# Loading the first k-tile in four transfers and holding back the fourth k-tile's load, in a two-layer decoder trunk

## The chip, the cores and the metric

The kernel runs on one core of a Trainium2 chip. The metric is the device time of one execution in microseconds (us), the median of several runs. The engines' names in the profile are PE (TensorE, the matmuls; PEld is its loading of weights), DVE (VectorE), ACT (ScalarE), POOL (GpSimd) and SP (SyncE, which here only issues transfers). A name with a q behind it (SPq, ACTq) is the engine's sequencer, which issues transfers and waits.

## What is computed

The reference is a decoder trunk of two layers on 256 tokens of 1024 features, in float32. In each layer a token mixer is followed by a dense MLP, and each of the two is added to its scaled input and normalised:

```
for i in range(DEPTH):                      # DEPTH = 2
    mix = moba_attention(h, ...) if i == 0 else dilated_attention(h, ...)
    h = layer_norm(ALPHA * h + mix, ...)
    h = layer_norm(ALPHA * h + square(relu(h @ w_in)) @ w_out, ...)
```

Layer 0 has 16 heads of causal attention (with 256 tokens there is one block of keys, so each query sees its own block alone); layer 1 has 12 heads in three groups of dilated windows. The MLP is 4096 wide. What matters here is the very first piece of work: `x @ w_qkv`, of which the first six blocks of 128 output columns, rotated later into queries and keys, are computed from a combined table `xw0` that holds, for each of the eight k-tiles of 128 features, the 256 columns of the transposed activations and then 768 columns of weights, 1024 columns in all (512 KB).

## The kernel before, in words

All matmuls keep nearly the precision of float32 with three products: each operand is split into a rounded part hi and the rest lo, and hi by hi, hi by lo and lo by hi are summed in PSUM. So each tile of weights that is loaded (`raw`) is first converted to hi (a copy that rounds, mostly on ACT, L355, or on DVE, L357) and then to lo (a subtraction on DVE, L360). The activations of a k-tile are converted in the same way into `xs`.

The start of the program is in the class `Stage` (L383), one object for each of the eight k-tiles of `xw0`. `STAGE_PARTS` (L54) says, for the first, second, third and all later k-tiles: into which parts the 1024 columns are cut (part 0 is the 256 columns of activations, the others are blocks of weights, given by the block at which each ends), which engine rounds each part of weights, and which parts are loaded by one transfer on which queue (SP's or ACT's). Before, the first k-tile is cut after weight blocks 1, 3 and 6; parts 0 and 1 (384 columns, 192 KB) come by one transfer on SP's queue, parts 2 and 3 (640 columns, 320 KB) by one on ACT's. The second k-tile comes half by SP and half by ACT, the third in two halves by SP, all later ones in a single transfer of 512 KB by SP. K-tiles 0 to 3 land in buffers of the tag `raw`; later ones borrow the buffers of `g`, `b` and `tok`.

The loop at L606 then makes 18 matmuls for each k-tile: three terms for each of six blocks of weights, into three PSUM banks (`acc`). Ahead of them stand dummy matmuls of 512 columns on constants (`WARM`, L60, eight of them, and `idle`, L455), which keep TensorE busy until data come; one more of 256 columns stands behind the first real matmul.

All operations are recorded with what they read and write, and then set into an order by a planner (`Plan.order`, L163) that simulates the engines with costs and due times. Each engine works off its own list in that order, and semaphores hold an instruction back until what it reads has been written. Transfers on one queue go out in the order in which they are issued; a transfer whose completion semaphore is still in use by an earlier one waits for that one to land (eight such semaphores take turns). SP's list at the start is: the first k-tile's part, the second's, two of the third, then the k-tiles four to eight, the rope table, two tiles of `wqk0`, and then all later weights.

Of the kernel before, what the change touches and what calls it, by code (L numbers as in the profile page):

```python
# [47 lines left out]
NFIRST = 6  # L48
PER = 1024 // (NFIRST * P)

STAGE_HOME = (("raw", NRAW),) * 4 + (("g", 1), ("b", 1)) + (("tok", 2),) * 2


STAGE_PARTS = (  # L54
    ((1, 3, NFIRST), ("DVE", "ACT", "ACT"), ((0, 1, "SP"), (2, 3, "ACT"))),
    ((2, NFIRST), ("DVE", "ACT"), ((0, 1, "SP"), (2, 2, "ACT"))),
    ((2, NFIRST), ("ACT", "ACT"), ((0, 1, "SP"), (2, 2, "SP"))),
    ((NFIRST,), ("ACT",), ((0, 1, "SP"),)),
)
WARM = (512,) * 8  # L60

# [51 lines left out]
class Plan:  # L115
# [16 lines left out]
    def op(self, eng, cost, fn, reads=(), writes=(), xfer=0.0, early=0.0, ahead=0.0):  # L132
        o = Op()
        o.n, o.eng, o.cost, o.fn, o.xfer = len(self.ops), eng, cost, fn, xfer
        o.early, o.ahead = early, ahead
        o.preds, o.succs, o.bufs = set(), [], set()
        for group, is_write in ((reads, False), (writes, True)):
            for item in group:
                b, key = item if isinstance(item, tuple) else (item, None)
                o.bufs.add(b)  # L140
                for k, st in b.state.items():
                    if key is None or k is None or k == key:
                        if st[0] is not None:
                            o.preds.add(st[0])
                        if is_write:
                            o.preds.update(st[1])
                st = b.state.setdefault(key, [None, []])
                if is_write:
                    if key is None:
                        b.state = {None: [o, []]}  # L150
                    else:
                        st[0], st[1] = o, []
                else:
                    st[1].append(o)
        o.preds.discard(o)
        for p in o.preds:
            p.succs.append(o)
        for b in o.bufs:
            b.left += 1
        self.ops.append(o)  # L160
        return o
# [133 lines left out]
def tile_trunk(  # L295
# [22 lines left out]
    nc = tc.nc  # L318
    plan = Plan()
    op = plan.op  # L320
# [5 lines left out]
    class Bufs:  # L326
        def __init__(self, pl, bufs):
            self.pl, self.bufs = pl, bufs
# [4 lines left out]
    def mk(shape, dt, tag, bufs, space=None):  # L333
        uid[0] += 1
        return plan.buf(Bufs(space or sb, bufs), shape, dt, tag, bufs, f"{tag}_{uid[0]}")

    def psum(tag):
        return mk([P, 512], F32, tag, 4, ps_pool)
# [14 lines left out]
    def split(n, src, hi, lo, r, whi, wlo, sbuf=False, hi_eng="ACT"):  # L353
        if hi_eng == "ACT":
            op("ACT", act(n, sbuf=sbuf), lambda: nc.scalar.activation(hi(), src(), AF.Copy), r, whi)  # L355
        else:
            op("DVE", dve(n), lambda: nc.vector.tensor_copy(hi(), src()), r, whi)  # L357
        op(
            "DVE", dve(n),
            lambda: nc.vector.tensor_tensor(lo(), src(), f32(hi()), op=ALU.subtract), list(r) + list(whi), wlo,  # L360
        )

    def mm(out_ap, lhsT, rhs, start, stop):
        nc.tensor.matmul(out_ap, lhsT, rhs, start=start, stop=stop)  # L364
# [16 lines left out]
    xs = [mk([P, 4, 2, S], F32R, f"xs{i}", 1) for i in range(2)]  # L381

    class Stage:  # L383


        def __init__(self, kt, hi, lo):
            self.kt, self.hi, self.lo = kt, hi, lo
            self.raw = mk([P, D], F32, *STAGE_HOME[kt])
            ends, self.engines, loads = STAGE_PARTS[min(kt, len(STAGE_PARTS) - 1)]
            cuts = [S] + [S + n * P for n in ends]  # L390
            self.parts = list(zip([0] + cuts[:-1], cuts))
            for first, last, eng in loads:
                self.load(self.parts[first][0], self.parts[last][1], tuple(range(first, last + 1)), eng)
            a, k = kt // 4, kt % 4
            keys = [(kt, m) for m in range(2)]
            split(
                S, lambda: self.raw.t[:, :S], lambda: xs[a].t[:, k, 0, :], lambda: xs[a].t[:, k, 1, :],
                [(self.raw, 0)], [(xs[a], (0, *m)) for m in keys], [(xs[a], (1, *m)) for m in keys], sbuf=True,
            )
            for i, (c0, c1) in list(enumerate(self.parts))[1:]:  # L400
                src = slice(c0, c1)
                dst = slice(self.col(0) + c0 - S, self.col(0) + c1 - S)
                split(
                    c1 - c0, lambda src=src: self.raw.t[:, src], lambda dst=dst: hi.t[:, dst],
                    lambda dst=dst: lo.t[:, dst], [(self.raw, i)], [(hi, (kt, i))], [(lo, (kt, i))], sbuf=True,
                    hi_eng=self.engines[i - 1],
                )
# [47 lines left out]
    def idle(n, reads=()):  # L455
        ones = nc.const_aps.tensor
        op(
            "PE", n / 2400, lambda: mm(idle_ps.t[:, :n], ones(1.0, [P, P], BF16), ones(1.0, [P, n], BF16), True, True),
            list(reads), [idle_ps],
        )  # L460

    for n in WARM:
        idle(n)

    stages = []
# [138 lines left out]

    first_ps = [psum("acc") for _ in range(NFIRST // 2)]
    for st in stages:  # L606
        for term in range(3):
            for j in range(NFIRST):
                st.mms(first_ps[j // 2], j, term)
                if st.kt == term == j == 0:  # L610
                    idle(256, [(st.hi, (0, 1)), (xs[0], (0, 0, 0))])


    turns = {"score": 0, "prob": 0}
# [696 lines left out]
```

## Time and profile before

| what | value |
|---|---|
| median of 3 runs | 559.67 us |
| the three runs | 559.62, 559.67, 560.46 us |
| the profiled execution | 560.61 us |
| its span in the profile | 558.8 us |
| TensorE busy | 551.1 us, 99% of the span |
| first dummy matmul | 0.77 us |
| first real matmul | 4.41 us |
| first matmul of the third k-tile | 9.98 us |
| first matmul of the fourth k-tile | 12.14 us |

Times in the profile count from the start of the span. A row of the timeline has the start, the duration, the engine, the line, the operation, what it writes and reads, the shape, and behind an x how many instructions of that kind were merged; in square brackets is how long the engine stood idle before it and what ended that. A matmul's busy time is modelled and overlaps the next one's, so the pace of TensorE is read from starts and counts, not from durations. The rows by window give the busy time and count of each engine in a stretch, the granted clock of TensorE, the share in which the 16 DMA engines were busy and the GB/s that they moved. A row of transfers gives the size and the time from issue until it had landed.

### The profile page before, as it was taken

Reading aid. Unit: us, or ns where it says so; the run is one execution under the profiler, and the core shown is the slowest. Engines: PE = TensorE matmul, PEld = TensorE weight load, DVE = VectorE, ACT = ScalarE, POOL = GpSimd, SP = SyncE. Lnnn points to the kernel's source line nnn. Section 1 sums busy time; section 2 is a strip of 40 time slices with the busy share of each in tenths; the row PEclk is TensorE's granted clock in tenths of the full one; section 3 lists DMA queues with packets and bytes.
Section 4 is the critical chain, followed back from the end, with each engine's and each line's share of the span. In section 5 each row is a group of like instructions: output and inputs, shape, how many; then the busy total and the mean of one; then the engine's idle time right before and its main releaser. Section 6 shows DMA issues by size and latency. Waiting matters only on the chain.

```text
span 558.8 us, 8590 instructions
## 1 busy us (share of the span) xinstructions
PE 551.1 (99%) x3236; PEld 470.8 (84%) x3236; DVE 412.4 (74%) x726; ACT 302.4 (54%) x492; POOL 9.2 (2%) x14
## 2 busy tenths in 40 slices
PE   9999999999999999999999999999999999999995
PEld 7988888888888888888888889888888888888884
DVE  6699999897674764855879899889848548558446
ACT  6467897257555555455534566556654554555400
POOL 0000000000000000000000000010000000000001
PEclk9999999999999999999999999999999999999999
DMA  8985245549884754745427535525967456463002
GB/s 330 410 308 190 73 155 201 213 124 309 260 283 146 254 177 163 232 172 198 143 121 250 186 105 178 189 75 178 310 228 261 159 184 225 154 223 114 1 0 76
DMA packets 30281, 105.61 MB, mean 189 GB/s; under 512 B 3360, under 2 KB 4256, under 8 KB 30240
## 3 DMA queue, kind: packets, MB, share of 16 engines
q1 hardware_dynamic: 29664, 104.35, 54.7%
q10 hardware_dynamic: 576, 0.72, 0.4%
q8 instruction: 25, 0.41, 0.3%
q14 instruction: 16, 0.13, 0.1%
HBM read 104.01 MB, written 1.05 MB: 188 GB/s over the span
## 4 chain that ended last, share of the span: by engine, by line
PE 98%; DMA 1%; DVE 0%; POOL 0%; DVEq 0%; ACT 0%; issue 0%; POOLq 0%
PE acc L364 59%; PE tp L364 36%; PE tp L693 3%; DMA raw<-in_xw_dram 1%; POOL rstd L807 0%; DVE tok L560 0%; DVEq L1305 0%; DVE bst L838 0%; ACT xs L355 0%; DVE mv L805 0%; POOLq L850 0%; POOLq L807 0%
## 5 line engine op out<-in xcount | busy, mean ns | idle before, releaser
L360 DVE TENSOR_TENSOR wlo<-raw,whi 128x1024 fp32r<-128x1024 f32 (+3 forms) x186 | 218.1, 1191 | 100.5 <-PE tp L364 59.0
L355 ACT ACTIVATE whi<-raw 128x1024 fp32r<-128x1024 f32 (+1 forms) x184 | 189.0, 1042 | 113.5 <-PE acc L364 67.9
L364 PE MATMUL acc<-whi,ahi 128*128 128x512 f32 (+1 forms) x312 | 121.6, 390 | 0.0
L364 PE MATMUL acc<-wlo,ahi 128*128 128x512 f32 (+1 forms) x312 | 121.0, 388 | 0.0
L364 PE MATMUL tp<-xs,whi 128*128 128x512 f32 x448 | 104.6, 390 | 0.0
L364 PE MATMUL acc<-whi,alo 128*128 128x512 f32 (+1 forms) x312 | 102.7, 387 | 0.0
L364 PEld LDWEIGHTS tp<-xs,whi 128*128 128x128 f32 x448 | 84.0, 188 | 17.3
L364 PEld LDWEIGHTS acc<-whi,alo 128*128 128x128 f32 x312 | 58.6, 188 | 12.1
L364 PEld LDWEIGHTS acc<-whi,ahi 128*128 128x128 f32 x312 | 58.7, 188 | 11.5 <-issue 0.3
L364 PEld LDWEIGHTS acc<-wlo,ahi 128*128 128x128 f32 x312 | 58.7, 188 | 11.2
L364 PE MATMUL acc<-xs,whi 128*128 128x512 f32 (+1 forms) x272 | 57.6, 360 | 0.1
L364 PEld LDWEIGHTS tp<-xs,wlo 128*128 128x128 f32 x448 | 55.6, 192 | 1.1
L364 PE MATMUL tp<-xs,wlo 128*128 128x256 f32 x448 | 55.9, 283 | 0.0
L364 PEld LDWEIGHTS acc<-xs,whi 128*128 128x128 f32 x272 | 45.3, 194 | 7.7 <-ACT xs L355 1.0
L355 ACT ACTIVATE ahi<-ta 128x256 fp32r<-128x256 f32 x56 | 23.4, 419 | 44.6 <-DVE ta L560 44.3
L932 ACT ACTIVATE ta<-tp 128x256 f32<-128x256 f32 x56 | 21.3, 380 | 26.2 <-PE tp L364 26.2
L553 DVE TENSOR_TENSOR ta<-tp,ta 128x256 f32<-128x256 f32 x56 | 23.4, 419 | 12.7 <-ACT ta L932 12.6
L364 PE MATMUL acc<-xs,wlo 128*128 128x256 f32 x224 | 30.4, 283 | 0.0
L364 PEld LDWEIGHTS acc<-xs,wlo 128*128 128x128 f32 x224 | 29.1, 191 | 0.9
L364 PE MATMUL acc<-whi,xs 128*128 128x512 f32 (+1 forms) x112 | 29.1, 367 | 0.0
L364 PE MATMUL tp<-whi,xs 128*128 128x512 f32 x80 | 25.2, 396 | 0.0
L560 DVE SCALAR_TENSOR_TENSOR ta<-ta 128x256 f32<-128x256 f32 x56 | 23.8, 425 | 1.8
(106 smaller groups left out, 465.5 us busy)
## 6 DMA issues: line engine op xcount, KB each, us to landing
raw<-in_win_dram SPq DMA_DIRECT2D x64, 512.0 KB, 4.3
raw<-in_wout_dram SPq DMA_DIRECT2D x64, 512.0 KB, 4.0
raw<-in_wqk_dram SPq DMA_DIRECT2D x22, 512.0 KB, 4.9
raw<-in_wo_dram SPq DMA_DIRECT2D x14, 512.0 KB, 4.2
raw<-in_wv_dram SPq DMA_DIRECT2D x8, 512.0 KB, 5.4
g<-in_lng_dram SPq DMA_DIRECT2D x4, 512.0 KB, 6.1
b<-in_lnb_dram SPq DMA_DIRECT2D x4, 512.0 KB, 6.3
raw<-in_wv1a_dram SPq DMA_DIRECT2D x4, 512.0 KB, 3.3
```

Of the source, the lines that this page charges most:

```text
L355: op("ACT", act(n, sbuf=sbuf), lambda: nc.scalar.activation(hi(), src(), AF.Copy), r, whi)
L360: lambda: nc.vector.tensor_tensor(lo(), src(), f32(hi()), op=ALU.subtract), list(r) + list(whi), wlo,
L364: nc.tensor.matmul(out_ap, lhsT, rhs, start=start, stop=stop)
L553: op("DVE", dve(n) + extra, lambda: nc.vector.tensor_tensor(out_ap(), a(), b(), op=alu), r, w)
L560: lambda: nc.vector.scalar_tensor_tensor(dst(), a(), s(), b(), op0=o0, op1=o1), r, w,
L693: nc.tensor.transpose(ps.t[:, c : c + P], src(), ident.t)
L932: op("ACT", act(S), lambda: nc.scalar.activation(u(), ps.t[:, S:], AF.Copy), [ps], uk)
```

## The change

The first k-tile's 1024 columns are cut after weight blocks 2, 4 and 6, so into four equal parts of 256 columns, and each comes by its own transfer of 128 KB: the activations and the second part of weights (blocks 2 and 3) on SP's queue, the first and the third part of weights on ACT's. The first part of weights is rounded by DVE, the other two by ACT, as before.

In the first k-tile TensorE's order puts all three terms of the first part's two blocks ahead of the other four blocks, and the extra dummy matmul stands behind the second real one. There are seven dummy matmuls at the start and not eight.

Ahead of the fourth k-tile's load GpSimd copies one column of the first k-tile's third part (`HELD_ON = 2`, counted from 0: weight blocks 0 and 1 are part 1, blocks 2 and 3 part 2) into the first column of the buffer that this load writes. The load, on SP, has to wait until the copy has been made, and the copy until that part has landed. All that SP issues later stands behind it.

```diff
+HELD, HELD_ON = 3, 2
 STAGE_PARTS = (
-    ((1, 3, NFIRST), ("DVE", "ACT", "ACT"), ((0, 1, "SP"), (2, 3, "ACT"))),
+    ((2, 4, NFIRST), ("DVE", "ACT", "ACT"), ((0, 0, "SP"), (1, 1, "ACT"), (2, 2, "SP"), (3, 3, "ACT"))),
     ((2, NFIRST), ("DVE", "ACT"), ((0, 1, "SP"), (2, 2, "ACT"))),
     ((2, NFIRST), ("ACT", "ACT"), ((0, 1, "SP"), (2, 2, "SP"))),
     ((NFIRST,), ("ACT",), ((0, 1, "SP"),)),
 )
-WARM = (512,) * 8
+WARM = (512,) * 7
...
             self.parts = list(zip([0] + cuts[:-1], cuts))
+            if kt == HELD:
+                raw, c = stages[0].raw, stages[0].parts[HELD_ON][0]
+                op("POOL", 0.1, lambda: nc.gpsimd.tensor_copy(self.raw.t[:, 0:1], raw.t[:, c : c + 1]), [(raw, HELD_ON)], [(self.raw, 0)])
             for first, last, eng in loads:
...
     for st in stages:
-        for term in range(3):
-            for j in range(NFIRST):
-                st.mms(first_ps[j // 2], j, term)
-                if st.kt == term == j == 0:
-                    idle(256, [(st.hi, (0, 1)), (xs[0], (0, 0, 0))])
+        n = STAGE_PARTS[0][0][0]
+        todo = sorted((st.kt > 0 or j >= n, term, j) for term in range(3) for j in range(NFIRST))
+        for _, term, j in todo:
+            st.mms(first_ps[j // 2], j, term)
+            if st.kt == term == 0 and j == n - 1:
+                idle(256, [(st.hi, (0, 1)), (xs[0], (0, 0, 0))])
```

## The prediction

> **What bounds the kernel now.** I read the page's engine row and chain first, then the chain of waits over the first 40 us, then every instruction of the first 14 us.
>
> ```profile
> span 558.8 us, 8590 instructions
> PE 551.1 (99%) x3236; PEld 470.8 (84%) x3236; DVE 412.4 (74%) x726; ACT 302.4 (54%) x492; POOL 9.2 (2%) x14
> PE 98%; DMA 1%; DVE 0%; POOL 0%; DVEq 0%; ACT 0%; issue 0%; POOLq 0%
> ...
> 0.74 3.18 DMA raw<-in_xw_dram
> ...
> 3.94 0.42 ACT xs L355
> ...
> 4.41 0.58 PE acc L364
> ...
> 5.22 23.44 PE acc L364 x175
> ```
>
> TensorE is the chain for 98% of the span. Ahead of it stand only one load (0.74 to 3.91 us) and one conversion (to 4.36). So whatever the change does, it does by when TensorE starts, how fast it then runs, and whether a later load makes it wait. The start in detail:
>
> ```profile
> 0.74 0.89 ACTq L351 DMA_DIRECT2D raw<-in_xw_dram  x2
> 0.74 2.29 SPq L351 DMA_DIRECT2D raw<-in_xw_dram  x5
> 0.77 3.57 PE L364 MATMUL tp<-const-bfloat16-1.0 128*128 128x512 bf16 x8 [0.77 <-PEq L1296]
> 0.98 0.55 POOL L448 TENSOR_TENSOR warm<-warm,expo 128x1 f32<-128x1 f32 x1 [0.54 <-DVE warm L446]
> 1.66 1.28 ACT L355 ACT_TABLE_LOAD   x1 [1.66 <-PEq L1296]
> 3.94 0.42 ACT L355 ACTIVATE xs<-raw 128x256 fp32r<-128x256 f32 x1 [0.99 <-DMA raw<-in_xw_dram]
> 4.26 0.81 ACT L355 ACTIVATE whi<-raw 128x256 fp32r<-128x256 f32 x2
> 4.41 0.42 DVE L360 TENSOR_TENSOR xs<-raw,xs 128x256 fp32r<-128x256 f32 x1
> 4.88 2.39 PE L364 MATMUL acc<-xs,whi 128*128 128x256 f32 x11
> 5.77 0.42 ACT L355 ACTIVATE xs<-raw 128x256 fp32r<-128x256 f32 x1 [0.70 <-DMA raw<-in_xw_dram]
> 5.78 0.29 DVE L357 CAST whi<-raw 128x256 fp32r<-128x256 f32 x1
> 7.10 0.88 PE L364 MATMUL acc<-xs,wlo 128*128 128x256 f32 x6
> 8.71 0.42 ACT L355 ACTIVATE xs<-raw 128x256 fp32r<-128x256 f32 x1 [0.64 <-DMA raw<-in_xw_dram]
> 9.03 0.83 ACT L355 ACTIVATE whi<-raw 128x768 fp32r<-128x768 f32 x1
> 9.98 1.60 PE L364 MATMUL acc<-xs,whi 128*128 128x256 f32 x12
> 12.14 1.60 PE L364 MATMUL acc<-xs,whi 128*128 128x256 f32 x12
> ```
>
> Two things are to be seen. First, the second k-tile's parts are converted from 5.77 and the fourth's from 8.71, but TensorE, 18 matmuls to a k-tile, comes to the third at 9.98 and to the fourth at 12.14: from the second k-tile on TensorE is late, not the data. Second, TensorE runs slowly at first. Between 4.88 and 7.10 it begins 11 matmuls (0.20 us each), between 7.10 and 9.98 another 24 (0.12 each). The granted clock reads 1.00 throughout; the counts of weight loads in two equal stretches show the change of pace:
>
> ```profile
> core 0: us, PEld busy (x), PEclk, DMA share, GB/s
> 5.24:6.72 1.48, 1.48 (x8) 1.00 0.96 329
> 7.11:8.59 1.48, 1.48 (x14) 1.00 1.02 415
> ```
>
> Less those cut by the edges, that is 0.21 us a matmul, then 0.12, with the turn near 6.7 us. The slow pace costs about 11 x 0.09 = 1.0 us here. The profiled execution took 560.61 us against 559.67 (the median), with the lowest run at 559.62: the spread is about this price, so I take it (an estimate) that in the two lower runs the turn came before the first real matmul. A rule of the Trainium skill bears on the row: "TensorE: Matmul & The Clock Gate", Part 1, says that the array runs at half clock until it has been busy for one window of about 3.4 us, and that the windows run freely, whatever the kernel does. By that rule the turn falls anywhere between one and two windows after the first matmul, 4.2 to 7.6 us here (an estimate from that page); the row's 6.7 agrees.
>
> **The change, part by part.**
>
> *Four transfers of 128 KB.* How fast bytes come:
>
> ```profile
> core 0: us, PE busy (x) PEld busy (x) DVE busy (x) ACT busy (x) POOL busy (x), PEclk, DMA share, GB/s
> 1.70:2.30 0.60, 0.60 (x3) 0.18 (x2) 0.00 (x0) 0.60 (x1) 0.00 (x0) 1.00 0.67 84
> 2.30:3.80 1.50, 1.50 (x5) 0.44 (x3) 0.00 (x0) 0.64 (x1) 0.00 (x0) 1.00 1.00 370
> 3.80:4.80 1.00, 0.94 (x4) 0.30 (x3) 0.83 (x4) 0.86 (x3) 0.00 (x0) 1.00 1.00 313
> 4.80:6.00 1.20, 1.20 (x7) 1.20 (x7) 1.09 (x4) 0.50 (x2) 0.00 (x0) 1.00 0.94 306
> ...
> raw<-in_xw_dram ACTq DMA_DIRECT2D x1, 320.0 KB, 3.4
> raw<-in_xw_dram SPq DMA_DIRECT2D x1, 192.0 KB, 3.2
> ```
>
> By 2.30 us some 50 KB have moved (0.6 x 84). The first 524 kB (192 and 320 KB) are through at 2.30 + (524 - 50)/370 = 3.58; they were usable at 3.94 (SP's) and 4.26 (ACT's, the first conversion of it), so 0.4 to 0.7 after the bytes. Now the activations and the first two weight blocks are 262 kB in two transfers side by side: through at 2.30 + 212/370 = 2.87, usable at 3.3 to 3.6. I take 3.5; the bounds are 3.3 and 3.94 (no sooner than now, if the slow stretch up to 2.3 us is per transfer and not per byte). The other two parts end with the same total bytes as now, about 4.26.
>
> *ACT issues three loads, not two.* At 0.89/2 = 0.45 each its table load moves from 1.66 to about 2.1 and ends at 3.4, just under the landing; cover gone if the data came before 3.4. SP's x5 above were the first four k-tiles; now five issues are the first three, and the second and third go out one issue (0.46) later.
>
> *Conversions.* The activations' conversion runs 3.50 to 3.92 in place of 3.94 to 4.36. VectorE converts 256 columns in one (0.29) instead of 128, done by 3.8. So the first real matmul starts 0.05 later, at 3.97 in place of 4.41: 0.44 earlier (0.6 and 0 at the bounds).
>
> *Seven warming matmuls, not eight, and a new order.* Eight dummies fill 0.77 to 4.34 (0.45 each), 0.07 short of the first real one; seven end at 3.9, again 0.07 short of 3.97. The one taken off costs nothing while the data come sooner; if they do not, the gap is 0.5. In the first k-tile all three terms of the first two blocks now come before the other four; TensorE's order is otherwise unchanged. After the first matmul and a dummy, the steady run began 0.81 later (the chain's 5.22); now at 4.78, and the low activations that it needs are there (VectorE 3.97 to 4.39, as 4.41 to 4.83 before). Then 0.21 each: by 6.73 it has begun 12 where it had begun 10. Two matmuls more at 0.12: **0.25 us** gained when the turn comes at 6.7. The late parts are converted by ACT from 4.26 in 0.81 as now, the first half of it well before its matmuls at about 5.6.
>
> When the turn comes early, TensorE runs at 0.12 and meets the data instead: the second k-tile's activations, 6.19 (5.77 + 0.42) if its load lands as now. Before would reach that k-tile at 7.1 (4.41 + 0.81 + 16 x 0.12), after at 6.7, and the nearer it comes to the data, the more it waits for that k-tile's later parts. Between 0 and 0.44; I take 0.2, the middle.
>
> *The hold.* A copy of one column on GpSimd waits for the third part (about 4.26). Its price is not shown; bounds: the 0.10 of a constant's memset and the 0.55 above.
>
> ```profile
> 0.24 0.10 POOL L1296 MEMSET const-float32-0.0<- 128x1 f32 x1 [0.24 <-issue]
> ...
> 3.06 0.44 SPq L351 DMA_DIRECT2D g<-in_xw_dram  x1
> 4.11 0.33 SPq L351 DMA_DIRECT2D b<-in_xw_dram  x1
> ...
> SPq L351 <- DMA raw<-in_xw_dram: 1.9, 4, 0.8
> ```
>
> I take 0.4 (it reads and writes, like the 0.55), so SP issues the fourth k-tile at about 4.75, not 2.6. Behind it on SP wait k-tiles five to eight, the rope table and two weight tiles; then each conversion of them on ACT and VectorE, and TensorE. What hides it: SP's queue still holds k-tiles one to three (1.5 MB), whose bytes at the rates above end near 6.7, and a load issued at 4.75 starts a good 1.0 later (the first, at 0.74, has moved little by the end of the 1.70 window's 0.6 us), 5.8. So the stream has no hole; even issued alone, with 3.2 of the 192 KB row and 320 KB more at 415 GB/s (0.79), it lands at 8.7, as now. TensorE needs it 1.2 of conversion (8.71 to 9.86) before 11.9: it may land at 10.7. Cover 2.0 us; beyond it each us costs one. SP already waits for earlier landings (the 1.9 us row, and the gap ahead of 4.11), so only the place of such a wait is new. "SBUF — State Buffer", section "SBUF: two separate sides" of the Trainium skill, says that GpSimd and a VectorE operation with two SBUF inputs shut each other out for a whole instruction; the copy may thus start one such operation later (0.42 in the rows above, an estimate). That is inside the cover, and no run here shows it yet.
>
> *Sum.* Profiled execution: 560.61 - 0.25 = 560.36. Median, by its earlier turn: 559.67 less 0.2 (early turn) to 0.25 = **559.4 us**. Later waits do not eat it: TensorE has no wait for another engine over 0.4 us after the first conversion.
>
> ```profile
> PEld acc L364 <- ACT xs L355: 1.0, 1, 1.0
> PEld acc L364 <- DVE xs L360: 0.4, 1, 0.4
> PEld tp L364 <- ACT sc L679: 0.4, 1, 0.4
> ```
>
> **The rivals.**
>
> - *The first data come no sooner*, or the second k-tile later by what the first gained (two more transfers are issued ahead of it). For it: the 84 GB/s stretch may belong to the transfers' start. Against: SP's 192 KB were usable before ACT's 320 KB, so size counts. Gain 0, with a gap of 0.5 in front: 559.7.
> - *The clock turns later (slower).* One dummy less leaves TensorE idle from 3.9 to the first data; if it then counts as idle, the turn comes later, and each us of delay costs 1 - 0.12/0.21 = 0.43 us. From an early turn to one after 7.5 us, some 15 slow matmuls at 0.09: +1.4 on 559.7, about 561.0. It decides from a delay of 2.6 us up (1.1/0.43). For it: the gap of 0.5 if the load is no sooner. Against: by the bounds above the load is sooner. That activity is the condition is the page's rule on the clock gate, named above; the trace shows only that the turn came.
> - *The hold uncovers the load stream (slower).* It decides only from a landing 2.0 us later than now; at 3.5 us it costs 1.5: 560.9. Against: every bound above is inside the cover.
> - *The hold also speeds the second k-tile (faster).* The stretch from 3.80 to 6.00 runs at 306 to 313 GB/s, the rest at 415. If queued loads caused that, 680 kB would take 1.64 and not 2.2: 0.56 sooner. With an early turn and the first data at their lower bound the gain is 0.6 + 0.56: 558.5; it decides from 1.1. Against: the loads held were behind the others in SP's own queue.
>
> **How the numbers follow.** Forecast 0.56 (own range 559.1 to 559.7), no gain 0.18, clock later 0.11, hold uncovered 0.04, second k-tile sooner 0.11. What a measurement of this kernel can tell from no change is about 0.2%, 1.1 us: below 558.55 is faster, above 560.8 slower. Forecast and no gain are both within: same 0.74, faster 0.11, slower 0.15. The range 558.5 to 560.7 takes in the faster case's lower end and runs whose turn comes late, and leaves out the two slower cases.
>
> **What would show it.** Right: the first conversion of activations starts near 3.5, the first real matmul near 3.97, seven dummies, the fourth k-tile issued on SP between 4.5 and 5.2 and converted before 10.7, TensorE never waiting after the third matmul. Wrong: the first landing still at 3.9; a turn of pace much after 7 us; a fourth k-tile converted after 10.9 with TensorE waiting for it; or a hole in the transfer rate near 6 us.

## The result: slower by a quarter of a per cent

The changed kernel took 561.41 us (median; 561.01 to 562.23) against 560.00 us for the kernel before, eight executions of each: a ratio of 1.0026, 95% interval 1.0017 to 1.0035. That is 1.4 us lost (1.0 to 2.0) where 0.25 us less was forecast, and it lies above the range.

The profiled execution of the changed kernel took 561.01 us. The head of its page:

```profile
span 559.2 us, 8595 instructions
PE 550.6 (98%) x3235; PEld 470.2 (84%) x3235; DVE 412.2 (74%) x726; ACT 302.4 (54%) x492; POOL 9.4 (2%) x15
```

and its chain in order of time (start, duration, what), at the start and where TensorE's last result leaves:

```profile
1.65 5.06 DMA raw<-in_xw_dram
...
6.73 0.43 ACT xs L357
...
7.20 21.26 PE acc L366 x158
...
551.79 0.02 issue
```

Before, TensorE's work on this chain began behind the first k-tile's load; now it begins behind the second's: the transfer that SP issues third, at 1.65, is through only 5.06 us later, and TensorE takes up the second k-tile at 7.20 when its activations have been converted. The same rows of the timeline as before:

```profile
0.73 1.38 ACTq L353 DMA_DIRECT2D raw<-in_xw_dram  x3
2.14 1.28 ACT L357 ACT_TABLE_LOAD   x1 [2.14 <-issue]
3.48 0.42 ACT L357 ACTIVATE xs<-raw 128x256 fp32r<-128x256 f32 x1
4.09 0.77 PE L366 MATMUL acc<-xs,whi 128*128 128x256 f32 x2 [0.17 <-DVE whi L359]
4.73 0.72 ACT L357 ACTIVATE whi<-raw 128x256 fp32r<-128x256 f32 x2 [0.83 <-DMA raw<-in_xw_dram]
4.76 0.18 POOL L397 COPY raw<-raw 128x1 f32<-128x1 f32 x1 [3.23 <-DMA raw<-in_xw_dram]
6.73 0.42 ACT L357 ACTIVATE xs<-raw 128x256 fp32r<-128x256 f32 x1 [1.27 <-DMA raw<-in_xw_dram]
7.20 0.30 PEld L366 LDWEIGHTS acc<-xs,whi 128*128 128x128 f32 x2 [0.43 <-ACT xs L357]
9.34 0.42 ACT L357 ACTIVATE xs<-raw 128x256 fp32r<-128x256 f32 x1 [0.53 <-DMA raw<-in_xw_dram]
9.77 1.60 PE L366 MATMUL acc<-xs,whi 128*128 128x256 f32 x12
11.93 1.60 PE L366 MATMUL acc<-xs,whi 128*128 128x256 f32 x12
```

The first activations are converted from 3.48 (3.94 before), the second k-tile's from 6.73 (5.77 before), and TensorE waits 0.43 for them. Yet it reaches the third k-tile at 9.77, not 9.98. That is luck of the two executions and no gain: in this one the pace turned early. The counts of weight loads in the stretch used before:

```profile
5.24:6.72 1.48, 1.48 (x15) 1.48 (x13) 0.70 (x2) 0.21 (x1) 0.00 (x0) 1.00 1.06 403
```

Thirteen where the kernel before had eight. So these two executions differ by the turn as well as by the change; the medians, and kernels below whose turn was early, tell the loss. (The profiled execution is also the shortest of the eight.) With an early turn and two first transfers, TensorE comes to the third k-tile at 8.98 to 9.43 and to the fourth at 11.14 to 11.59; here it was 9.77 and 11.93. So 0.3 to 0.8 us are lost at the start of this execution.

The rest is lost at the other end. TensorE's last result leaves at 551.79, 0.20 before that of the kernel before (551.99), but the span ends 0.4 later (559.2 against 558.8). In the stretch from 556 to 557.2 us the transfers of the changed kernel are (queue: packets, MB, share; then an issue with KB and us to landing):

```profile
q14 instruction: 1, 0.01, 3.9%
out_dram<-tok ACTq DMA_DIRECT2D x1, 64.0 KB, 2.5
```

and of the kernel before, in the same stretch:

```profile
out_dram<-tok ACTq DMA_DIRECT2D x1, 64.0 KB, 2.0
```

The last store takes 2.5 us and not 2.0, and beside it runs a load of 8 KB of instructions (by the trace's records it starts 0.65 us after that store is issued; before, 2.02 after it, when the store has all but landed). From the last matmul's start to the end of the span it is 7.72 us in place of 7.14. This is the tail in what follows.

The hole at the start is seen in the transfer rates (the last column, GB/s), in the stretches that the prediction used:

```profile
1.70:2.30 0.60, 0.60 (x3) 0.18 (x2) 0.00 (x0) 0.16 (x1) 0.00 (x0) 1.00 0.45 96
2.30:3.80 1.50, 1.50 (x4) 0.30 (x2) 0.15 (x1) 1.44 (x2) 0.00 (x0) 1.00 1.03 288
3.80:4.80 1.00, 0.83 (x5) 0.65 (x4) 0.90 (x3) 0.17 (x2) 0.04 (x1) 1.00 0.76 228
4.80:6.00 1.20, 1.20 (x12) 1.20 (x11) 0.76 (x2) 0.65 (x2) 0.14 (x1) 1.00 1.01 367
```

Before, 2.30 to 4.80 ran at 370 and 313. Rate by time, the kernel before had moved 0.6 x 84 + 1.5 x 370 + 1.0 x 313 = 918 kB by 4.80 us, the changed one 0.6 x 96 + 1.5 x 288 + 228 = 718.

### The profile page after: what moved, and what is told of

Read it like the earlier page. It is cut to its first block, busy times and chain, and to the rows that moved or that the text cites. A ratio compares the mean times of both kernels' runs of the same rounds, so it can differ in the third digit from the quotient of the medians.

```text
span 559.2 us, 8595 instructions
## 1 busy us (share of the span) xinstructions
PE 550.6 (98%) x3235; PEld 470.2 (84%) x3235; DVE 412.2 (74%) x726; ACT 302.4 (54%) x492; POOL 9.4 (2%) x15
## 4 chain that ended last, share of the span: by engine, by line
PE 97%; DMA 1%; DVE 0%; POOL 0%; SPq 0%; DVEq 0%; ACT 0%; issue 0%; POOLq 0%
PE acc L366 58%; PE tp L366 36%; PE tp L701 3%; DMA raw<-in_xw_dram 1%; POOL rstd L815 0%; DVE tok L566 0%; SPq L353 0%; DVEq L1313 0%; DVE bst L846 0%; ACT xs L357 0%; DVE mv L813 0%; POOLq L858 0%; POOLq L815 0%
## 5 line engine op out<-in xcount | busy, mean ns | idle before, releaser
L362 DVE TENSOR_TENSOR wlo<-raw,whi 128x1024 fp32r<-128x1024 f32 (+2 forms) x186 | 217.9, 1190 | 100.9 <-PE tp L366 53.1
```

## The experiments

Theory after the result: four transfers ahead of the second k-tile delay it, and the hold and the missing dummy cost nothing. Rivals: the hold; the dummy; the address pattern; the size of the pieces; the third load on ACT's queue. And for the tail: the length of some engine's program.

### Each part of the change alone

Without the hold:

```diff
-            if kt == HELD:
+            if False:
```

> The changed kernel without the hold: the fourth k-tile's load waits for no copy; the four transfers, the new order and seven dummies stay. Theory (four small transfers bring the second k-tile late, TensorE waits for it, and a code load in the tail costs 0.5): the second k-tile's conversion still starts near 6.7 us, TensorE begins the third k-tile near 9.8, time 561.0 to 561.5; if the tail's code load moves with the two instructions fewer, some 0.5 less. Rival (the hold is the cost): second k-tile's conversion back near 5.8, time at 560.0 or below. Rival (the missing dummy): 561.4.

The kernel before with the hold alone:

```diff
+            if kt == 3:
+                raw, c = stages[0].raw, stages[0].parts[2][0]
+                op("POOL", 0.1, lambda: nc.gpsimd.tensor_copy(self.raw.t[:, 0:1], raw.t[:, c : c + 1]), [(raw, 2)], [(self.raw, 0)])
```

> The kernel before with the hold alone: one column of the first k-tile's part 2 is copied by GpSimd into the fourth k-tile's buffer, so its load and all later ones on SP wait until that part has landed. Theory (transfers and tail): first conversion 3.94 and second k-tile's conversion 5.8 as before, TensorE as before, time 559.9 to 560.2, or up to 560.6 if the instructions added bring the code load into the tail. Rival (the hold is the cost): 561 or more. Rival (the missing dummy): 560.0.

The changed kernel with two transfers, of 256 KB each:

```diff
-    ((2, 4, NFIRST), ("DVE", "ACT", "ACT"), ((0, 0, "SP"), (1, 1, "ACT"), (2, 2, "SP"), (3, 3, "ACT"))),
+    ((2, 4, NFIRST), ("DVE", "ACT", "ACT"), ((0, 1, "SP"), (2, 3, "ACT"))),
```

> The changed kernel with the first k-tile in two transfers of 256 KB (parts 0 and 1 on SP, 2 and 3 on ACT); cuts, order, hold and seven dummies stay. Theory: the first conversion is back near 3.9 to 4.0, the second k-tile's back near 5.8 to 6.0, no wait of TensorE ahead of the second k-tile; time 560.0, or 560.5 with the code load in the tail. Rival (the hold): 561.4. Rival (the missing dummy): 561.4.

The changed kernel with eight dummies:

```diff
-WARM = (512,) * 7
+WARM = (512,) * 8
```

> The changed kernel with eight dummy matmuls at the start and not seven. Theory: the eighth dummy ends near 4.3 us, after the data of the first matmul are there, so TensorE starts some 0.2 later, but it waits for the second k-tile at 7.2 all the same; time 561.4 as without it. Rival (the missing dummy delays the clock): back to 560.0 to 560.4.

| kernel | median, us (before beside it: 560.09) | ratio and interval | second k-tile's activations converted from (one execution) |
|---|---|---|---|
| no hold | 561.69 | 1.0028 (1.0017 to 1.0039) | 8.04 |
| hold alone | 559.90 | 0.9999 (0.9991 to 1.0008) | 5.30 |
| two transfers | 560.11 | 1.0014 (1.0004 to 1.0025) | 5.80 |
| eight dummies | 561.64 | 1.0025 (1.0014 to 1.0036) | 7.71 |

The loss stays without the hold and with eight dummies, and the hold alone costs nothing. Only with the four transfers gone does the second k-tile come back, and by the median the loss is gone (560.11); the ratio keeps half of it. Of twelve executions with two transfers seven stand near 560.0 and five at 561.3 to 562.2, which pulls its ratio up; what those five were is open, since the profiled execution was one of the seven. That one shows, however, a rest of TensorE before its first real matmul:

```profile
4.56 0.50 PE L366 MATMUL acc<-xs,whi 128*128 128x256 f32 x2 [0.64 <-ACT xs L357]
```

The seventh dummy ends at 3.92, and with two transfers the first data come later than that. This is the gap that the prediction named as the condition of its rival "the clock turns later", and the two equal halves below, with eight dummies, have no such gap and no execution over 560.48. So the five may be late turns of the clock; no run separates the dummy from the new order here.

The kernel without the hold was expected to lose 0.5 less if the load of code at the end moved. It did move (tail 7.22), yet the kernel takes 561.69 us: here the start alone costs some 1.5 (1.60 less 0.08 of tail). With four transfers the hold may thus have helped, but these runs do not show it. The timeline of this kernel shows the wait plainest:

```profile
8.04 0.42 ACT L357 ACTIVATE xs<-raw 128x256 fp32r<-128x256 f32 x1 [2.58 <-DMA raw<-in_xw_dram]
...
8.51 0.96 PE L366 MATMUL acc<-xs,whi 128*128 128x256 f32 x4 [1.18 <-ACT xs L357]
```

### Addresses, pieces or transfers

The changed kernel, rows of the first matrix 4352 bytes apart and not 4096:

```diff
-    d["xw0"] = np.concatenate([x.T.reshape(KT, P, S), qk[:, :n].reshape(KT, P, n)], axis=2)
+    d["xw0"] = np.concatenate([x.T.reshape(KT, P, S), qk[:, :n].reshape(KT, P, n), np.zeros((KT, P, 64), f)], axis=2)
```

> The changed kernel, with 64 unused columns behind each row of the first matrix, so that rows start 4352 bytes apart and not 4096. If the address pattern (equal 1024-byte pieces at a power-of-two distance) is what delays the second k-tile: its activations' conversion starts at 5.3 to 6.0, the time is that of the kernel before, 559.8 to 560.3. If the number of transfers or the size of their pieces delays it: the conversion stays at 6.7 to 8.0 and the time at 561.2 to 561.7.

Measured 561.77 us, ratio 1.0033 (1.0022 to 1.0045), the conversion from 7.44. The address pattern is not it.

The kernel before with two equal halves:

```diff
-    ((1, 3, NFIRST), ("DVE", "ACT", "ACT"), ((0, 1, "SP"), (2, 3, "ACT"))),
+    ((2, 4, NFIRST), ("DVE", "ACT", "ACT"), ((0, 1, "SP"), (2, 3, "ACT"))),
```

> The kernel before, with its two first transfers cut at the middle (256 KB each, pieces of 2048 bytes in place of 1536 and 2560). No other part of the change. If pieces that are equal and divide the row evenly are the trouble, a part of the executions is late as with two transfers in the changed order: a median of 560.0 to 560.6 with single executions at 561.3 to 562.2. If they are not: all at 559.7 to 560.5, the second k-tile's conversion at 5.3 to 6.0.

Measured 560.15 us, ratio 1.0002 (0.9993 to 1.0011), the conversion from 5.50, no execution over 560.48. This kernel is the base of the next two. First, its two transfers in twice as many pieces (the first k-tile lies in runs of 256 columns with 16 unused between them):

```diff
+            if self.kt == 0:
+                dst = lambda: self.raw.t[:, c].rearrange("p (a n) -> p a n", n=256)
+                src = xw0[0].rearrange("p (a n) -> p a n", n=272)[:, c0 // 256 : c1 // 256, :256]
```

> The kernel with equal halves, two transfers of 256 KB as there, but the first k-tile lies in memory in runs of 1024 bytes with 64 bytes between them, so that the two transfers have 512 pieces of 1024 bytes. If the number of pieces delays the second k-tile: its conversion starts at 6.7 to 8.0 and the time is 560.7 to 561.7. If the number of transfers does: 5.3 to 6.0 and 559.8 to 560.5.

Measured 559.76 us, ratio 0.9997 (0.9988 to 1.0006). The row of the timeline with its second k-tile's activations:

```profile
5.46 0.42 ACT L355 ACTIVATE xs<-raw 128x256 fp32r<-128x256 f32 x1 [0.61 <-DMA raw<-in_xw_dram]
```

and its rows by window:

```profile
2.30:3.80 1.50, 1.50 (x5) 0.44 (x3) 0.01 (x1) 0.79 (x2) 0.00 (x0) 1.00 1.06 370
3.80:4.80 1.00, 1.00 (x5) 0.45 (x3) 0.85 (x3) 1.00 (x3) 0.00 (x0) 1.00 1.12 350
```

The same 512 pieces of 1 KB as the changed kernel, and no hole. Second, the same 256 pieces in four transfers, each half cut by rows:

```diff
-    ((2, 4, NFIRST), ("DVE", "ACT", "ACT"), ((0, 1, "SP"), (2, 3, "ACT"))),
+    ((2, 4, NFIRST), ("DVE", "ACT", "ACT"), ((0, 1, "SP"), (2, 3, "ACT"), (0, 1, "SP"), (2, 3, "ACT"))),
...
+            r = slice(h * P // halves, (h + 1) * P // halves)
-                lambda: self.raw.t[:, c], xw0[self.kt][:, c], (), [(self.raw, i) for i in keys],
+                lambda: self.raw.t[r, c], xw0[self.kt][r, c], (), [(self.raw, (i, h)) for i in keys],
```

> The kernel with equal halves, each half cut once more, by rows: four transfers of 64 rows by 2048 bytes, the same 256 pieces ahead of the second k-tile as with two transfers (four column parts make 512 pieces). If the number of transfers delays the second k-tile: its activations' conversion starts at 6.7 to 8.0 and the time is 560.7 to 561.7. If the number of pieces does: 5.3 to 6.0 and 559.8 to 560.5.

Measured 563.33 us (561.91 to 564.44 in five executions), ratio 1.0069 (1.0055 to 1.0082), over the upper end. The profiled execution is the shortest of the five. Its rows of the timeline:

```profile
4.80 1.28 ACT L355 ACT_TABLE_LOAD   x1 [4.80 <-DMA raw<-in_xw_dram]
6.10 0.42 ACT L355 ACTIVATE xs<-raw 128x256 fp32r<-128x256 f32 x1
...
6.57 0.38 PE L364 MATMUL acc<-xs,whi 128*128 128x256 f32 x1 [2.22 <-ACT xs L355]
```

and its rows by window:

```profile
2.30:3.80 1.50, 1.50 (x5) 0.44 (x3) 0.00 (x0) 0.00 (x0) 0.00 (x0) 1.00 0.99 265
3.80:4.80 1.00, 0.55 (x2) 0.00 (x0) 0.00 (x0) 0.00 (x0) 0.00 (x0) 1.00 0.73 191
...
7.00:9.00 2.00, 2.00 (x19) 2.00 (x18) 1.93 (x7) 1.18 (x4) 0.00 (x0) 1.00 0.91 341
```

TensorE rested 2.22 us before its first real matmul. Part of that is a side effect: here ACT's table load stood waiting for the data and came behind them (1.28 us), where otherwise it runs ahead. But the rates are those of the hole, 265 and 191, the first half itself was usable at 4.80 in place of 3.9, and the second k-tile's activations are converted from 7.03. Its time says less than its rates: two of the five executions (563.18 and 563.33 us) have a mean granted clock of 0.993 and the others 0.996 to 0.998, a loss of another kind that the last section takes up. By the rates, the number of transfers decides, not the number or size of pieces.

### How many, on which queue, and ahead or behind

Three transfers (SP 128 KB, ACT 128 KB, SP 256 KB) in the kernel before:

```diff
-    ((1, 3, NFIRST), ("DVE", "ACT", "ACT"), ((0, 1, "SP"), (2, 3, "ACT"))),
+    ((2, 4, NFIRST), ("DVE", "ACT", "ACT"), ((0, 0, "SP"), (1, 1, "ACT"), (2, 3, "SP"))),
```

> The kernel before, with the first k-tile in three transfers: 128 KB on SP, 128 KB on ACT, then 256 KB on SP; cuts as in the changed kernel, ACT issues two loads and not three, no hold, eight dummies. If the number of transfers delays the second k-tile in proportion: its conversion starts at 6.2 to 6.7, the first real matmul at 4.0 to 4.1, the time 560.0 to 560.8. If the third load on ACT's queue, ahead of the second k-tile's, is what delays it: the conversion starts at 5.3 to 5.9 and the time is 559.4 to 560.0. If pieces of 1024 bytes do it whatever their number: 6.7 or later, 561.2 to 561.7.

Measured 560.84 us, ratio 1.0019 (1.0011 to 1.0028), the conversion at 6.65 (it stands behind another of ACT's). By then TensorE had already waited 1.26 us for the first k-tile's own late part, so in this execution the loss falls there and not on the second k-tile:

```profile
5.97 1.40 PE L364 MATMUL acc<-xs,whi 128*128 128x256 f32 x9 [1.26 <-ACT whi L355]
```

The fourth transfer on SP:

```diff
-(2, 2, "SP"), (3, 3, "ACT"))),
+(2, 2, "SP"), (3, 3, "SP"))),
```

> The changed kernel with the fourth transfer on SP behind the third, so that ACT issues two loads as before. If three loads on ACT's queue are what delays the second k-tile: its conversion comes back to 5.3 to 6.0 and the time to 559.6 to 560.3. If four transfers delay it on whichever queue: 6.7 to 8.0. ACT's program is one instruction shorter than in the changed kernel: if its length decides when the code load near the end comes, that load stands 1.3 us or more behind the last store's issue and the tail after the last matmul is 7.1 to 7.25, so 560.8 to 561.2 with a late second k-tile.

Measured 560.75 us, ratio 1.0011 (1.0002 to 1.0019), the conversion at 6.71: four transfers are late with two loads on ACT's queue too. Its rows by window:

```profile
2.30:3.80 1.50, 1.50 (x4) 0.29 (x2) 0.27 (x1) 1.06 (x2) 0.00 (x0) 1.00 1.13 263
3.80:4.80 1.00, 0.94 (x5) 0.76 (x5) 0.78 (x3) 0.00 (x0) 0.00 (x0) 1.00 0.77 198
```

One transfer of 512 KB:

```diff
-((0, 1, "SP"), (2, 3, "ACT"))),
+((0, 3, "SP"),)),
```

> The kernel before with the first k-tile in one transfer of 512 KB on SP, so that one transfer and not two stands ahead of the second k-tile. If each transfer ahead delays it: its conversion starts at 4.9 to 5.5. If two are as good as one, by bytes alone: 5.3 to 5.8. The first conversion starts later in either case, at 4.2 to 4.6 in place of 3.9, and the time is 559.9 to 560.6.

Measured 562.53 us, ratio 1.0045 (1.0033 to 1.0057), a miss: the one transfer was usable only at 5.38, and the second k-tile's conversion (6.94) stood behind it on ACT, so this kernel says nothing of a delay by transfers. Beside the one transfer on SP ran ACT's half of the second k-tile, issued at 0.73 and landed 4.8 later, and the bytes moved by 4.80 us are those of two transfers (table below): the first k-tile shared the rate with the second. What else made it dear is told in the last section.

Two small loads (16 KB each, never used) in the kernel before, one on each queue, behind the first k-tile's; then each alone:

```diff
+            if kt == 0:
+                for i, eng in enumerate(("SP", "ACT")):
+                    spare = mk([P, 32], F32, f"spare{i}", 1)
+                    dma(lambda spare=spare: spare.t, ident_in[:, 32 * i : 32 * i + 32], (), [spare], P * 32 * 4, eng)
```

> The kernel before, with two unused loads of 16 KB (128-byte pieces) issued right behind the first k-tile's two, one on each queue, so that four transfers stand ahead of the second k-tile as in the changed kernel. If the number of transfers delays the second k-tile: its conversion starts at 6.7 or later and the time is 561 to 561.6. If the size of the pieces of the first k-tile's own transfers does: the conversion stays at 5.3 to 6.0 and the time at 559.8 to 560.3.

> The kernel before with one unused load of 16 KB on SP, between the first k-tile's transfer and the second's. If one more transfer ahead of it on its own queue delays the second k-tile: its activations' conversion starts at 6.7 or later, and the time is 560.1 to 560.5. If the load on ACT's queue did it in the run with two small loads: 5.3 to 6.2 (one issue of 0.46 later at the most) and 559.8 to 560.2.

> The kernel before with the unused load of 16 KB on ACT alone, which goes out behind ACT's part of the second k-tile. If a third load on ACT's queue, even a small one behind, delays the second k-tile (it was scattered from 6.7 to 8.0 in the kernels with three there): its conversion starts at 6.5 or later. If only transfers ahead on the same queue count: 5.3 to 5.8 and 559.8 to 560.2.

Both: 560.33 us, ratio 1.0006 (0.9998 to 1.0015), and in the timeline

```profile
7.17 0.42 ACT L355 ACTIVATE xs<-raw 128x256 fp32r<-128x256 f32 x1 [0.89 <-DMA raw<-in_xw_dram]
```

TensorE waits 0.47 us for this conversion. The small load on ACT's queue was issued third there, behind ACT's part of the second k-tile, so three transfers and not four stand ahead. The second k-tile is late as expected, the time below the 561 expected.

On SP alone, ahead of the second k-tile: 560.32 us, ratio 1.0007 (0.9998 to 1.0016), and a conversion between the two ranges expected:

```profile
6.42 0.42 ACT L355 ACTIVATE xs<-raw 128x256 fp32r<-128x256 f32 x1 [0.27 <-DMA raw<-in_xw_dram]
```

On ACT alone, where it goes out behind that queue's part of the second k-tile: 559.94 us, ratio 1.0001 (0.9993 to 1.0010), and

```profile
5.42 0.42 ACT L355 ACTIVATE xs<-raw 128x256 fp32r<-128x256 f32 x1 [0.54 <-DMA raw<-in_xw_dram]
```

So 16 KB, a thirtieth of the first k-tile, put the second back by 0.65 to 1.4 us when they stand ahead of it on its queue, of which one issue explains 0.47; behind it on the other queue they do nothing. These are single executions, and in the kernels with two transfers the conversion itself starts anywhere from 5.30 to 5.80. In time this is worth some 0.4 us, at the edge of what can be told, since the second k-tile has slack here.

Does what is queued behind it count? The hold was moved to the third k-tile, with four transfers (the fourth on SP) and with two:

```diff
-HELD, HELD_ON = 3, 2
+HELD, HELD_ON = 2, 2
```

> The changed kernel with the fourth transfer on SP, and the hold on the third k-tile's two loads in place of the fourth's. If transfers queued behind the second k-tile's share the channel with it and delay it: its conversion comes back from 6.7 to 5.3 to 6.2, and the time to 559.6 to 560.2. If only those ahead of it count: 6.5 to 7.2 and 560.6 to 561.0, as with the fourth transfer on SP alone.

> The kernel before (two first transfers) with the third k-tile's two loads held until the first k-tile's third part has landed. If queued loads delay the second k-tile: its conversion starts at 4.9 to 5.4 in place of 5.3 to 5.8, and the time is 559.4 to 559.9. If they do not: 5.3 to 5.8 and 559.7 to 560.2. If the third k-tile then comes late (issued at about 4.8, landing near 7.5, needed near 9): a wait for it, 560.3 or more.

Four transfers: 561.96 us, ratio 1.0035 (1.0023 to 1.0047); the second k-tile is as late as ever, though until 5.63 only its own two transfers and the first k-tile's were under way (rows of the timeline, the second, third and fourth k-tile):

```profile
6.68 0.42 ACT L357 ACTIVATE xs<-raw 128x256 fp32r<-128x256 f32 x1
8.26 0.42 ACT L357 ACTIVATE xs<-raw 128x256 fp32r<-128x256 f32 x1 [1.16 <-DMA raw<-in_xw_dram]
12.04 0.42 ACT L357 ACTIVATE xs<-raw 128x256 fp32r<-128x256 f32 x1 [1.93 <-DMA raw<-in_xw_dram]
```

Two transfers: 560.60 us, ratio 1.0010 (1.0001 to 1.0018), the second k-tile at 5.39, a value that lies in both ranges expected and so decides nothing. In both the hold one k-tile earlier empties the queue, and the fourth k-tile comes at 12.04 and 11.33: here a hold does uncover the stream. By the pair with four transfers (6.68 here, 6.71 with the hold on the fourth k-tile), what is queued behind the second k-tile is not what delays it; what stands ahead is.

All kernels side by side, by the bytes moved until 4.80 us, worked out as above from the rows of the same three stretches, one execution each:

| transfers ahead of the second k-tile | kB by 4.80 us |
|---|---|
| one | 922 |
| two (before, hold alone, two in the changed order, equal halves, small pieces, small on ACT, hold on the third, later loads on ACT) | 918, 1022, 939, 1019, 1024, 1018, 997, 961 |
| three (small on SP, two small, three loads) | 870, 838, 790 |
| four (changed, no hold, padded, fourth on SP, hold on the third, rows) | 718, 697, 723, 678, 716, 629 |
| four (eight dummies) | 844 |

The last stands apart because its hole came later: its rate was 195 GB/s from 4.80 to 6.00. A hole is also in kernels with two transfers; in the one with equal halves it is in the second of these rows by window:

```profile
3.80:4.80 1.00, 0.91 (x5) 0.33 (x4) 0.68 (x3) 0.84 (x3) 0.00 (x0) 1.00 1.03 348
4.80:6.00 1.20, 1.20 (x13) 1.20 (x12) 1.20 (x6) 0.70 (x3) 0.00 (x0) 1.00 0.82 217
```

and there it falls on the third k-tile (converted from 7.58, and needed by TensorE from 8.98), which has time. With more transfers ahead the hole mostly comes sooner, and the second k-tile pays, which has little. The runs do not tell the two queues apart: with three of the four on SP the second k-tile is converted from 6.71, with two on each from 6.73 in the changed kernel and as late as 8.04 without the hold.

### The tail

The changed kernel's ACT issues one load more and the hold adds an instruction: the trace has 708 instructions on ACT, 706 before. The kernel before with two unused loads on ACT's queue, issued with the eighth k-tile:

```diff
+            if kt == 7:
+                for i, eng in enumerate(("ACT", "ACT")):
+                    spare = mk([P, 32], F32, f"spare{i}", 1)
+                    dma(lambda spare=spare: spare.t, ident_in[:, 32 * i : 32 * i + 32], (), [spare], P * 32 * 4, eng)
```

> The kernel before with two unused loads of 16 KB on ACT's queue, issued with the eighth k-tile, behind the start: ACT's program is then two instructions longer, as in the changed kernel, and nothing else is. If that length places the code load near the end: it comes 0.6 to 0.7 us behind the last store's issue, the tail after the last matmul is 7.65 to 7.75, and the time 0.4 to 0.6 above the kernel before, 560.3 to 560.7. If something else places it: a tail of 7.1 to 7.25 and 559.7 to 560.2.

Measured 560.57 us against 560.05, ratio 1.0010 (1.0002 to 1.0019), tail 7.72. From 556 to 557.2 us its transfers show the same two rows as the changed kernel's: one load of instructions, and a store of 64 KB that takes 2.5. The start is not quite untouched, though: ACT issues the two loads at 1.67, ahead of its table load (2.63 in place of 1.66), and the first real matmul starts at 4.61 in place of 4.41. So the 0.52 of the medians need not all be the tail; the tail itself is 0.58 longer in the traces (7.72 against 7.14).

The collision comes back with the length of ACT's program. All kernels agree: with 708 instructions on ACT (changed, eight dummies, padded, this one) the code load starts 0.65 to 0.70 us after the last store's issue and the tail is 7.69 to 7.73; with 706 or 707 it starts 1.32 or more after, and the tail is 7.02 to 7.23; with 709 (rows) it comes 1.0 ahead of that issue, and the tail is 7.25.

## Why the prediction was wrong

- **The step that failed** is "The other two parts end with the same total bytes as now, about 4.26", and with it "6.19 (5.77 + 0.42) if its load lands as now". Both took the rates of the trace before (370 and 313 GB/s) as a property of the bytes. With four transfers ahead they are 288 and 228: the third part was usable at 4.73, the fourth had landed at about 4.9 (issued at 1.18, 3.8 to landing), and the second k-tile's activations were there at 7.15. The first of the two fails only at times: with eight dummies and with padded rows these parts were converted from 4.10 and 3.87. The second fails in every kernel with four transfers (the conversion starts at 6.68 to 8.04). The 4.26 was itself read from a conversion that stood behind another of ACT's; by the prediction's row of transfers that load had landed at about 4.1 (0.74 + 3.4). By the prediction's own early-turn sum TensorE would have reached that k-tile at 6.7, 0.5 us after 6.19. That slack was for a load as early as now; the load came 0.96 later in the profiled execution (2.3 in the kernel without the hold).
- The rival that named the mechanism, the second k-tile "later by what the first gained (two more transfers are issued ahead of it)", had 0.18 and the wrong size: it was priced as a gain cancelled and no more. It is dearer than the gain: the fourth transfer on SP, which has four transfers and the old tail, costs 0.70 us (560.75 against 560.05).
- "Later waits do not eat it" failed twice: at 7.20 (0.43, for the second k-tile) and at the end, where nothing was looked for. The tail is 0.52 by the medians of the run that brings it about. 0.70 + 0.52 = 1.2 of the 1.4 measured, inside its interval. The first of these terms varies: without the hold, with a tail near the old one, the start costs some 1.5.
- First parts at 3.5: right, 3.48, with the table load just ahead (it ends at 3.42). With two loads on ACT's queue, where the table load ends at 2.94, the conversion starts at 3.33 to 3.39, so the table load leaves no cover. In the kernel with padded rows the first transfer had landed by about 3.3 (issued at 0.74, 2.5 to landing), and the conversion waited for the table load until 3.44.
- First real matmul at 3.97: 4.09, since VectorE's rounding of the first part of weights started at 3.65 and not by 3.5. A gain of 0.32 rather than 0.44, given away at the second k-tile.
- Seven dummies: right with four transfers, where eight changed nothing (561.64). With two transfers the seventh ends 0.64 before the first real matmul, and the price of that gap is open.
- The hold: right. The copy took 0.18 (0.4 assumed), the fourth k-tile was converted from 9.34 (10.7 allowed), and the hold alone has a ratio of 0.9999. That the cover is real shows where it is gone, with the hold on the third k-tile. The VectorE operation that keeps the copy waiting did not come up in this execution: VectorE was idle from 4.70 to 5.18, and the copy ran from 4.76 to 4.94. Other kernels show it. Where a VectorE subtraction was under way when the copy began (hold alone, eight dummies, padded rows, the kernel before with the hold on the third k-tile), the copy took 0.25 to 0.45 and ended 0.04 to 0.05 after that subtraction; in the four others it took 0.18. Spans on GpSimd are rough in the profile, but all eight agree. So the prediction's allowance for such a wait was sound, and at most 0.3 of it was needed. In the kernel with padded rows:

```profile
3.88 0.43 DVE L362 TENSOR_TENSOR xs<-raw,xs 128x256 fp32r<-128x256 f32 x1
3.90 0.45 POOL L397 COPY raw<-raw 128x1 f32<-128x1 f32 x1 [2.37 <-DMA raw<-in_xw_dram]
```

- Two paces with a turn at a time of its own: right. An early turn goes with a low time, as the prediction took it: with equal halves, at 559.62 us, 14 weight loads start in the stretch where the kernel before had eight. It also masked the loss in the two profiled executions. No later turn was seen in the changed kernel, of which one execution, the shortest, was profiled.
- That the hold speeds the second k-tile: 5.30 against 5.77 in one execution each, and no time from it with two transfers. With four it is 6.73 against 8.04, and 7.44 and 7.71 in two other kernels with the hold, so this stays open.

No kernel here beats the one before by more than can be told; the best, with small pieces, has a ratio of 0.9997. Why an added transfer opens the hole (what an engine waits for while others are queued) is not shown by any run.

## What to carry to other kernels

At the start of a kernel count the transfers ahead of each load and not only the bytes, and look at the next tile's slack before cutting the first one finer: here the first data came 0.46 us sooner and the next came 1 to 2 us later, where half a microsecond of slack was reckoned with. A rate read from one arrangement of transfers is no rate for another. And when a change alters an engine's number of instructions, look at the end of the trace too: where a code load meets the last store, two instructions cost half a microsecond.

## What was not expected of the hardware

The code load at the end: with 8 KB of instructions loaded beside it, a store of 64 KB lands in 2.5 us in place of 2.0. The Trainium skill, "Runtime: NRT & Kernel Launch", section "Instruction fetch mechanics", says that an engine's sequencer fetches its next block of instructions by a DMA queue of its own and that the cost is mostly hidden; the trace agrees on the queue and shows one place where it is not hidden, since nothing after the last store covers it.

The clock can fall again after a short rest. With one transfer of 512 KB TensorE stood still for 1.73 us, and then (a row of the timeline, then rows by window, in which the granted clock is the last number but two):

```profile
5.84 0.38 PE L364 MATMUL acc<-xs,whi 128*128 128x256 f32 x1 [1.73 <-ACT xs L355]
```

```profile
7.00:9.00 2.00, 2.00 (x12) 2.00 (x11) 2.00 (x7) 1.88 (x7) 0.00 (x0) 0.54 1.02 414
9.00:11.00 2.00, 2.00 (x13) 2.00 (x12) 2.00 (x4) 1.90 (x4) 0.00 (x0) 0.61 1.03 422
11.00:13.00 2.00, 2.00 (x19) 2.00 (x18) 2.00 (x5) 1.78 (x4) 0.00 (x0) 1.00 1.02 413
```

The clock is at 0.54 and 0.61 in these four microseconds, in which 23 weight loads start where 36 would: 13 x 0.11 = 1.4 us, on top of the late start (5.84 in place of 4.41). That is close to the rival "the clock turns later": TensorE rests and then runs slowly, though here the clock falls after it had turned (from 6 to 7 us eight weight loads start, the fast pace). It does not follow each time. The mean granted clock over the span is 0.993 in this execution and in one other of the six, and 0.996 to 0.999 in the rest; the fall takes 2 x 0.46 + 2 x 0.39 = 1.7 us of clock, 0.003 of the span, so by this mean it came in two of the six. The kernel cut by rows rested 2.22 us in its profiled execution and kept its clock (1.00 from 7 to 9 us, above), while two of its five executions have 0.993 as well. So the length of the rest alone does not decide; what does is not shown. The Trainium skill, "TensorE: Matmul & The Clock Gate", Part 1, has windows of about 3.4 us that run freely and a fall after an idle one; a fall after 1.73 us of rest is sooner than that, by this trace.
